# Host layouts, split input weights, idle matmuls and a new step order at the head of a hybrid decoder layer

## The chip, the cores and the metric

The kernel runs on one core of one Trainium2 chip. The metric is the time of one execution on the device in microseconds (us), smaller is better. Arrays that the host lays out before the launch are not in it.

The names of the engines in the profile: PE is TensorE (matmuls; PEld its weight loads), DVE VectorE, ACT ScalarE, POOL GpSimd, SP the engine that issues nearly all DMAs. SPq, ACTq and so on are the instruction queues of these engines. L127 is line 127 of the kernel.

## What is computed

One layer of a decoder trunk, for 2048 prompt rows and 64 sample rows (8 sequences of 8 positions), with shared weights, all in float32:

```
h = rmsnorm(x, g_pre_mix)
q, k, v, u = split(h @ w_in)              # 1024 -> 512 + 128 + 128 + 512 columns
attn   = window attention of rope(q), rope(k), v, window 128, one sink logit per head
pooled = (trailing mean of u over 2/4/8/16 positions - u) @ pool_w, times pool_scale
mix = concat(rmsnorm(attn, g_attn_out), rmsnorm(pooled, g_pool_out)) @ w_out
x += rmsnorm(mix, g_post_mix)
x += rmsnorm(relu(rmsnorm(x, g_pre_mlp) @ w_up)**2 @ w_down, g_post_mlp)
x += sigmoid(x @ w_ple_gate + b) * (p @ w_ple)
```

The sample rows attend to 128 past keys and values per sequence (state_k, state_v), and their pooling starts from the last 15 pooled inputs (state_pool). New keys, values and pooled inputs are outputs as well.

## The kernel before, in words

Every float32 product is made of three products of split operands (mm3, L132 to L136): an operand is rounded to a shorter format (its high part, a copy on ScalarE) and what is left is its low part (a subtraction on VectorE, lo_of, L129). high x high, high x low and low x high are added up in PSUM. So a weight matrix has to be loaded, scaled, copied and subtracted before it can be multiplied.

The first 440 us or so hold everything up to the input of w_out. The rows come in tiles of 128; the 64 sample rows are tile -1, the prompt rows tiles 0 to 15.

*Loading and splitting.* queue (L125) is a DMA that keeps its place in the order of SP's queue. load_gains (L286) loads norm weights as eight rows of 128, turns them with a TensorE transpose (gps, L296) and copies them into gains: the eight columns of g_pre_mix at the start, the eight of g_attn_out and g_pool_out in tile 2. load_w_in (L320) loads 128 rows of w_in with all 1280 columns (raw, six buffers), scales them by g_pre_mix and writes the high part (L324, ScalarE) and the low part (L325, VectorE). head (L347) loads the rows x of a tile, their transposed form xt, and the rotary table cs, and forms the norm factor; split_head (L370) splits xt into hT.

*front* (L380) is a tile's product with w_in, in eight steps of 128 rows (k): kvps (keys and values, 256 columns), qps (512), ups (512), then rotary work, transposes of keys and queries (trk, trq) and copies. For tile -1 the three products run together, step by step, as w_in arrives. Its past keys (sk) and pooled inputs (su) are turned on TensorE (trk L660 in sample_attention, trs L571 in pooling).

*attention* (L485) works in six steps (a): scores and softmax for each of two key groups, then for each group the transposes of the weights (trp, L541) with their split (pt), and the product with the values (po, L551 and L552). *pooling* (p) has three steps, *finish* (l) two. *split_w_out* (e, L751) loads w_out in pieces (wraw), scales them by g_attn_out or g_pool_out (L767, L768; wsp has one buffer) and stores the split form in device memory (wod); it belongs to tiles 3 to 10.

*The order of the work.* The main loop weaves, for each tile t, the attention and pooling of t with the front of t + 1 (f) and the finish of t - 1. A string of letters says in which order the next steps are taken: ORDER (L44) for tiles 0 to 2 and 11 to 13, called plain tiles here, ORDERW (L46) for tiles 3 to 10, ORDER1 and ORDER2 for 14 and 15. What this gives is the program's order; the framework then places instructions on each engine's queue by its own model of time, so that an instruction whose inputs it takes to be ready can be put ahead of one that stands earlier in the program. On the chip each queue is worked off in order.

After this part come the product with w_out, the two large products with w_up and w_down, and the gate; the change does not touch them.

Of the kernel before, what the change touches and what calls it, by code (L numbers as in the profile page):

```python
# [10 lines left out]
F32 = mybir.dt.float32  # L11
# [3 lines left out]
ALU = mybir.AluOpType  # L15
PSUM = bass.MemoryType.PSUM

P = 128
# [7 lines left out]
HD = 64  # L26
# [16 lines left out]

ORDER = "a f f f l f a f f p a f f f f f a f p f a f f l f p a"  # L44

# [43 lines left out]
def trunk(ctx: ExitStack, tc: tile.TileContext, i: dict, o: dict):  # L89
# [184 lines left out]
    with ExitStack() as sa:  # L274
# [10 lines left out]

        def load_gains(names, c0):  # L286
            graw = pa.tile([8, P], F32, tag="r", bufs=1, name="graw", padded_shape=[8, 512])
            r = 8 // len(names)
            for k, name in enumerate(names):
                rows = graw[k * r : (k + 1) * r]  # L290
                if name == "g_attn_out":
                    queue(rows.rearrange("k (g p) -> k g p", g=2), i[name][0].rearrange("(g k p) -> k g p", g=2, p=HD))
                else:
                    queue(rows, i[name][0].rearrange("(k p) -> k p", p=P))
            gps = tr.tile([P, 8], F32, tag="tr", name="gps", padded_shape=[P, 512])
            T.transpose(gps, graw, ident[:8, :8])  # L296
            V.tensor_copy(gains[:, c0 : c0 + 8], gps)

# [20 lines left out]

        def load_w_in(k):  # L320
            raw = over.pool.tile([P, INC], F32, tag="raw", bufs=6, name="raw")
            queue(raw, w_in[k * P : (k + 1) * P, :])
            g = gpre[:, k : k + 1]
            A.mul(out=wi[k][:, 0], in_=raw, mul=g)  # L324
            V.scalar_tensor_tensor(out=wi[k][:, 1], in0=raw, scalar=g, in1=wi[k][:, 0].bitcast(F32), op0=ALU.mult, op1=ALU.subtract)  # L325

        def load_pool_w():
            raw = over.pool.tile([P, INC], F32, tag="raw", bufs=6, name="raw")
            pr = raw[:, 0:512].rearrange("p (g d) -> p g d", g=4)
            SY.dma_start(pr, i["pool_w"][0].rearrange("g c d -> c g d"))  # L330
            SY.dma_start(raw[:, 512:1024], i["pool_scale"].to_broadcast([P, 512]))
            V.tensor_tensor(out=pr, in0=pr, in1=raw[:, 512:1024].rearrange("p (g d) -> p g d", g=4), op=ALU.mult)
            A.copy(out=pw[:, 0], in_=pr)
            lo_of(pw[:, 1], pr, pw[:, 0])
# [45 lines left out]
        def front(t, hT, cs, rs, res):  # L380
# [62 lines left out]
            yield  # L443
            if t >= 0:
                ups = mmp.tile([P, 512], F32, tag="mm", name="ups")
            for j, _ in enumerate(gemm(768, 512, ups) if t >= 0 else ()):
                yield
                if j == 0:
                    kp = over.pool.tile([P, 4, 256], F32R, tag="kp", bufs=2, name="kp")
# [110 lines left out]
        def pooling(t, u, mix, sq):  # L560
# [5 lines left out]
            if t < 0:  # L566
                sp = past[2]
                ns = NDEC * HALO
                ps = tr.tile([P, 4, P], F32, tag="tr", name="trs")
                for g in range(4):  # L570
                    T.transpose(ps[:, g, :ns], sp[:ns, g * P : (g + 1) * P], ident[:ns, :ns])  # L571
                V.tensor_copy(ux[:, :, :, :HALO], ps[:, :, :ns].rearrange("p g (b j) -> p g b j", b=nb))
            elif t == 0:
# [63 lines left out]

        def load_past():
            sp = over.pool
            sks = []  # L640
            for j in range(2):
                sk = sp.tile([P, 4, P], F32, tag="sk", bufs=2, name="sk")
                queue(sk, i["state_k"][0, 4 * j : 4 * j + 4].rearrange("b s g d -> s b (g d)"))
                sks.append(sk)
            su = sp.tile([P, 512], F32, name="su")
            queue(su[: NDEC * HALO], i["state_pool"][0].rearrange("b j c -> (b j) c"))
            sv = sp.tile([P, NDEC, P], F32, tag="raw", bufs=6, name="sv", padded_shape=[P, NDEC, 160])
            queue(sv, i["state_v"][0].rearrange("b s g d -> s b (g d)"))
            return sv, sks, su

        def sample_attention(kr, vr, qr, mix, sq):
            n = NS
            sp = over.pool
            sv, sks, _ = past
            kT = sp.tile([P, NDEC, P], F32, tag="raw", bufs=6, name="kT", padded_shape=[P, NDEC, 160])
            for j in range(2):
                sk = sks[j]
                ps = tr.tile([P, 4, P], F32, tag="tr", name="trk")
                for c in range(4):
                    T.transpose(ps[:, c, :], sk[:, c, :], ident)  # L660
# [129 lines left out]
        for t in range(-1, NT):  # L790
# [725 lines left out]
```

## Time and profile before

| | us |
|---|---|
| median of three runs | 2169.63 |
| lowest, highest | 2165.42, 2170.01 |
| the profiled execution, its own time | 2167.38 |
| span of its profile (first to last instruction) | 2165.6 |
| TensorE busy in it | 2127.1 |
| VectorE busy | 1581.1 |
| ScalarE busy | 958.5 |

The profile is of one execution. "Busy" of an engine is time in which an instruction of it runs; a matmul's end is modelled, and consecutive matmuls overlap, so that the distance from one start to the next tells their pace better than their durations. A wait is put down to the instruction whose signal came last. Rows in order of time give start, duration, engine, line, operation, out <- in, shapes and count, and in brackets the idle time of the engine before and what ended it.

### The profile page before, as it was taken

How to read it: one execution, taken by the hardware profiler on the slowest of the kernel's cores; microseconds unless marked ns; L12 is line 12 of the kernel's file. 1: busy time of each engine (PE TensorE's matmuls, PEld its weight loads, DVE VectorE, ACT ScalarE, POOL GpSimd, SP SyncE). 2: the span in 40 equal slices, each digit the busy share in tenths (PEclk: the TensorE clock that was granted, in tenths of full speed). 3: DMA queues.
4: the chain of work that ended last, by engine and by line, in shares of the span. 5: the costliest groups of instructions: out<-in, count | busy, mean ns of one | idle time of the engine just before them, and what ended most of it. 6: DMA issues, size and time to landing. Idle time of an engine off the chain costs nothing.

```text
span 2165.6 us, 31185 instructions
## 1 busy us (share of the span) xinstructions
PE 2127.1 (98%) x11435; PEld 1879.0 (87%) x11435; DVE 1581.1 (73%) x2716; ACT 958.5 (44%) x1856; POOL 566.7 (26%) x642
## 2 busy tenths in 40 slices
PE   8999999899999999999999999999999999999999
PEld 6888888777889999999999988788888888888887
DVE  6789999866688777555755566788888888876553
ACT  4667666635455445444544455233233233232221
POOL 2334443233341000000000035535535544300000
PEclk9999999999999999999999999999999999999999
DMA  6254312667879768766766632322231232342211
GB/s 209 75 178 164 96 62 89 238 209 219 258 247 309 239 211 272 206 192 187 228 199 191 180 111 78 111 84 65 90 100 49 90 100 62 117 138 83 88 54 40
DMA packets 309634, 320.43 MB, mean 148 GB/s; under 512 B 79526, under 2 KB 257906, under 8 KB 302281
## 3 DMA queue, kind: packets, MB, share of 16 engines
q1 hardware_dynamic: 309481, 318.44, 46.6%
q8 instruction: 90, 1.47, 0.3%
q14 instruction: 63, 0.52, 0.1%
HBM read 217.17 MB, written 102.51 MB: 148 GB/s over the span
## 4 chain that ended last, share of the span: by engine, by line
PE 81%; DVE 7%; DMA 4%; issue 3%; POOL 3%; ACT 2%; SPq 1%; POOLq 0%; ACTq 0%; DVEq 0%
PE up L1060 9%; PE up L1062 9%; PE up L1061 9%; PE dn L1276 9%; PE dn L1278 9%; PE dn L1277 9%; PE pg L136 3%; PE pg L135 3%; PE pg L134 3%; PE ups L134 1%; PE ups L136 1%; PE ups L135 1%; PE qps L135 1%; PE qps L134 1%; PE qps L136 1%
## 5 line engine op out<-in xcount | busy, mean ns | idle before, releaser
L1286 DVE TENSOR_TENSOR z<-dn,z 128x512 f32<-128x512 f32 x416 | 278.0, 684 | 77.7 <-PE dn L1278 69.8
L130 DVE TENSOR_TENSOR g<-raw,g 128x512 fp32r<-128x512 f32 x336 | 226.9, 694 | 89.6 <-ACT g L207 88.7
L1060 PE MATMUL up<-e,g 128*128 128x352 f32 x832 | 269.8, 325 | 5.1 <-ACT snap L1067 5.0
L1061 PE MATMUL up<-e,g 128*128 128x352 f32 x832 | 268.3, 322 | 0.0
L1062 PE MATMUL up<-e,g 128*128 128x352 f32 x832 | 264.5, 324 | 0.0
L207 ACT CAST g<-raw 128x512 fp32r<-128x512 f32 x336 | 203.9, 623 | 97.8 <-PE up L1062 78.0
L1225 POOL TENSOR_TENSOR raws<-raws 128x1024 f32<-128x1024 f32 x32 | 83.9, 2632 | 615.7 <-DVE wr L130 408.5
L1276 PE MATMUL dn<-wr,ms 128*128 128x512 f32 x512 | 199.3, 390 | 1.4 <-DVE z L1286 1.4
L1277 PE MATMUL dn<-wr,ms 128*128 128x512 f32 x512 | 199.2, 389 | 0.0
L1278 PE MATMUL dn<-wr,ms 128*128 128x512 f32 x512 | 198.2, 389 | 0.0
L1060 PEld LDWEIGHTS up<-e,g 128*128 128x128 f32 x832 | 157.0, 189 | 6.1 <-ACT snap L1067 5.6
L1061 PEld LDWEIGHTS up<-e,g 128*128 128x128 f32 x832 | 157.8, 190 | 0.1
L1062 PEld LDWEIGHTS up<-e,g 128*128 128x128 f32 x832 | 156.0, 189 | 0.0
L1074 DVE TENSOR_TENSOR t<-up,snap 128x352 f32<-128x352 f32 x144 | 71.3, 520 | 114.7 <-ACT snap L1067 101.0
L207 ACT CAST m<-fr 128x512 fp32r<-128x512 f32 (+1 forms) x128 | 65.4, 514 | 194.2 <-PE dn L1278 169.2
L1276 PE MATMUL dn<-wr,m 128*128 128x512 f32 x384 | 149.5, 389 | 1.7 <-DVE z L1286 1.7
L1277 PE MATMUL dn<-wr,m 128*128 128x512 f32 x384 | 149.4, 389 | 0.0
L1278 PE MATMUL dn<-wr,m 128*128 128x512 f32 x384 | 149.3, 389 | 0.0
L856 POOL TENSOR_TENSOR s<-fr 128x256 f32<-128x256 f32 x64 | 54.1, 845 | 309.6 <-DVE ms L130 238.7
L1067 ACT COPY snap<-up 128x352 f32<-128x352 f32 x144 | 61.0, 454 | 165.7 <-PE up L1062 165.6
L207 ACT CAST wr<-raws 128x1024 fp32r<-128x1024 f32 x66 | 69.2, 1052 | 114.7 <-PE dn L1278 57.8
L1276 PEld LDWEIGHTS dn<-wr,ms 128*128 128x128 f32 x512 | 96.1, 188 | 21.8 <-issue 1.8
(285 smaller groups left out, 5707.6 us busy)
## 6 DMA issues: line engine op xcount, KB each, us to landing
raw<-in_w_up_dram SPq DMA_DIRECT2D x160, 256.0 KB, 3.9
raw<-upt SPq DMA_DIRECT2D x32, 1024.0 KB, 7.9
fr<-ffd SPq DMA_DIRECT2D x64, 512.0 KB, 3.5
ffd<-r SPq DMA_DIRECT2D x96, 256.0 KB, 2.7
upt<-raw SPq DMA_DIRECT2D x16, 1024.0 KB, 5.2
raws<-in_w_down_dram SPq DMA_DIRECT2D x32, 512.0 KB, 5.4
sp<-hfd SPq DMA_DIRECT2D x21, 704.0 KB, 6.2
x<-in_x_prompt_dram SPq DMA_DIRECT2D x16, 512.0 KB, 4.5
```

The source lines that it names most:

```text
L130: eng.tensor_tensor(out=out, in0=full, in1=hi.bitcast(F32), op=ALU.subtract)
L134: T.matmul(ps, lhs[0], rhs[0], start=first, stop=False)
L135: T.matmul(ps, lhs[0], rhs[1], start=False, stop=False)
L136: T.matmul(ps, lhs[1], rhs[0], start=False, stop=last)
L207: copy(out=dst[:, 0], in_=src)
L1060: T.matmul(ps, l[0], r[0], start=st, stop=False, skip_group_check=not fresh)
L1061: T.matmul(ps, l[0], r[1], start=False, stop=False, skip_group_check=not fresh)
L1062: T.matmul(ps, l[1], r[0], start=False, stop=c == 3, skip_group_check=not fresh)
L1276: T.matmul(ps, l[0], r[0], start=fresh and j == 0, stop=False, skip_group_check=not fresh)
L1277: T.matmul(ps, l[0], r[1], start=False, stop=False, skip_group_check=not fresh)
L1278: T.matmul(ps, l[1], r[0], start=False, stop=j == 1, skip_group_check=not fresh)
L1286: V.tensor_tensor(out=z, in0=ps, in1=z, op=ALU.add)
```

## The change

- The host lays out three things: all sixteen columns of norm weights in one array (gains_t), the past keys transposed (state_kt), and the past pooled inputs transposed (state_pt). The kernel loads each with one DMA; load_gains and the transposes trk (L660) and trs (L571) with their copies are gone. The past pooled inputs are copied into place by GpSimd instead of VectorE.
- w_in is loaded in two column parts per 128 rows: columns 0 to 767 (q, k, v) of all eight row blocks first, then columns 768 to 1279 (u). raw has nine buffers of 768 columns instead of six of 1280.
- The transposed sample rows are loaded in two halves, between the first pieces of w_in.
- For tile -1 kvps and qps run together, ups afterwards.
- spin: before the first load is there, TensorE makes 18 transposes of the identity into a PSUM tile that nobody reads.
- The transposed rows of tile 0 are loaded ahead of its rows x, with the past keys, the constants and the sinks in between; past pooled inputs and values come after.
- ORDER is another string.

```diff
-ORDER = "a f f f l f a f f p a f f f f f a f p f a f f l f p a"
+ORDER = "f f f f l f a f f p a f f f f f a f p f a f f l a a p"
...
+        queue(gains, i["gains_t"])
+
+        def spin(k):
+
+            ps = tr.tile([P, 4, P], F32, tag="tr", name="spin")
+            for j in range(k):
+                T.transpose(ps[:, j % 4, :], ident, ident)
...
-        def load_w_in(k):
-            raw = over.pool.tile([P, INC], F32, tag="raw", bufs=6, name="raw")
-            queue(raw, w_in[k * P : (k + 1) * P, :])
+        def load_w_in(k, part):
+
+            c0, cw = (0, 768) if part == 0 else (768, 512)
+            raw = over.pool.tile([P, cw], F32, tag="raw", bufs=9, name="raw", padded_shape=[P, 768])
+            queue(raw, w_in[k * P : (k + 1) * P, c0 : c0 + cw])
             g = gpre[:, k : k + 1]
-            A.mul(out=wi[k][:, 0], in_=raw, mul=g)
-            V.scalar_tensor_tensor(out=wi[k][:, 1], in0=raw, scalar=g, in1=wi[k][:, 0].bitcast(F32), op0=ALU.mult, op1=ALU.subtract)
+            hi, lo = (wi[k][:, h, c0 : c0 + cw] for h in range(2))
+            A.mul(out=hi, in_=raw, mul=g)
+            V.scalar_tensor_tensor(out=lo, in0=raw, scalar=g, in1=hi.bitcast(F32), op0=ALU.mult, op1=ALU.subtract)
...
             if t < 0:
+                for j in range(2):
+                    js = slice(4 * j, 4 * j + 4)
+                    queue(xt[:, js, :n], x_t[:, js, c0 : c0 + n])
+                    load_w_in(j, 0)
+                for k in range(2, 5):
+                    load_w_in(k, 0)
+            if t == 0:
                 queue(xt[:, :, :n], x_t[:, :, c0 : c0 + n])
-                for k in range(2):
-                    load_w_in(k)
+                load_past(0)
+                queue(ct, i["consts"])
+                load_sinks()
             x = fp.tile([P, D], F32, tag="x", bufs=1, name="x")
             queue(x[:n], xrows(t))
-            if t >= 0:
+            if t > 0:
                 queue(xt[:, :, :n], x_t[:, :, c0 : c0 + n])
...
-                ups = op.tile([P, 512], F32, tag="o", name="ups")
-                for _ in zip_longest(gemm(512, 256, kvps, 1), gemm(0, 512, qps, 1), gemm(768, 512, ups, 1)):
+                for _ in zip_longest(gemm(512, 256, kvps, 1), gemm(0, 512, qps, 1)):
                     pass
...
-                for g in range(4):
-                    T.transpose(ps[:, g, :ns], sp[:ns, g * P : (g + 1) * P], ident[:ns, :ns])
-                V.tensor_copy(ux[:, :, :, :HALO], ps[:, :, :ns].rearrange("p g (b j) -> p g b j", b=nb))
+                G.tensor_copy(ux[:, :, :, :HALO], past["u"].rearrange("p g (b j) -> p g b j", b=nb))
...
-            for j in range(2):
-                sk = sks[j]
-                ps = tr.tile([P, 4, P], F32, tag="tr", name="trk")
-                for c in range(4):
-                    T.transpose(ps[:, c, :], sk[:, c, :], ident)
-                V.tensor_copy(kT[:, 4 * j : 4 * j + 4, :], ps)
-                yield
+            kT, sv = past["k"], past["v"]
...
-        load_gains(["g_pre_mix"], 0)
+        spin(18)
         heads[-1] = head(-1)
         split_head(-1)
-        for k in range(2, 8):
-            load_w_in(k)
+        for k in range(5, 8):
+            load_w_in(k, 0)
+        for k in range(8):
+            load_w_in(k, 1)
         heads[0] = head(0)
-        past = load_past()
-        queue(ct, i["consts"])
-        load_sinks()
+        load_past(1)
...
-            if t == 2:
-                load_gains(["g_attn_out", "g_pool_out"], 8)
```

More of the change, by code (lines that the diff above doesn't have):

```diff
@@ L284, in trunk @@
         mmp = sw.enter_context(tc.tile_pool(name="mmp", bufs=2, space=PSUM))
[L286 to L297, printed above, removed]
+        queue(gains, i["gains_t"])
[3 more added lines that the diff above has]
+                T.transpose(ps[:, j % 4, :], ident, ident)
         ct = ca.tile([P, C_COLS], F32, name="ct")
@@ L443, in front @@
             yield
-            if t >= 0:
-                ups = mmp.tile([P, 512], F32, tag="mm", name="ups")
-            for j, _ in enumerate(gemm(768, 512, ups) if t >= 0 else ()):
+            ups = mmp.tile([P, 512], F32, tag="mm", name="ups") if t >= 0 else op.tile([P, 512], F32, tag="o", name="ups")
+            for j, _ in enumerate(gemm(768, 512, ups)):
                 yield
+                if t < 0:
+                    continue
                 if j == 0:
@@ L636, in finish, with load_past @@
             SY.dma_start(mixd[t], mix[:, :, :n])
-        def load_past():
+        past = {}
+        def load_past(part):
             sp = over.pool
-            sks = []
-            for j in range(2):
[L642 to L649, printed above, removed]
+            if part == 0:
+                past["k"] = sp.tile([P, NDEC, P], F32, name="kT")
+                queue(past["k"], i["state_kt"])
+                return
+            past["u"] = sp.tile([P, 4, NDEC * HALO], F32, name="su")
+            queue(past["u"], i["state_pt"])
+            past["v"] = sp.tile([P, NDEC, P], F32, name="sv")
+            queue(past["v"], i["state_v"][0].rearrange("b s g d -> s b (g d)"))
         def sample_attention(kr, vr, qr, mix, sq):
@@ L1504 @@
     given["p_t"] = np.ascontiguousarray(p_all.T)
+    g_pre, g_attn, g_pool = (given.pop(n)[0] for n in ("g_pre_mix", "g_attn_out", "g_pool_out"))
+    g_attn = g_attn.reshape(2, 4, HD).transpose(0, 2, 1).reshape(P, 4)
+    given["gains_t"] = np.ascontiguousarray(np.concatenate([g_pre.reshape(8, P).T, g_attn, g_pool.reshape(4, P).T], axis=1))
+    given["state_kt"] = np.ascontiguousarray(given["state_k"][0].reshape(NDEC, WIN, P).transpose(2, 0, 1))
+    given["state_pt"] = np.ascontiguousarray(given["state_pool"][0].reshape(NDEC * HALO, 4, P).transpose(2, 1, 0))
     del given["p_prompt"], given["p_sample"]
```

14 lines of the change are left out of this document (4 added, 10 removed).

## The prediction

> **What bounds the kernel now.** I read the page first, then the waits of TensorE, then the busy time by stretches of the first 404 us, and then the first 27 us in order of time. The page shows one engine near its limit:
>
> ```profile
> span 2165.6 us, 31185 instructions
> PE 2127.1 (98%) x11435; PEld 1879.0 (87%) x11435; DVE 1581.1 (73%) x2716; ACT 958.5 (44%) x1856; POOL 566.7 (26%) x642
> L1225 POOL TENSOR_TENSOR raws<-raws 128x1024 f32<-128x1024 f32 x32 | 83.9, 2632 | 615.7 <-DVE wr L130 408.5
> ```
>
> TensorE (PE) is busy for 2127.1 of 2165.6 us, so no edit outside its idle 38.5 us gains unless it shortens TensorE's own work. The waits say where the idle time is (columns: who waited for whom, us in all, times, longest):
>
> ```profile
> PE kvps L134 <- ACT wi L324: 5.2, 1, 5.2
> ...
> PE trp L541 <- DVE pr L531: 3.9, 1, 3.9
> ...
> PE trk L453 <- DVE pt L130: 2.2, 1, 2.2
> PE trp L541 <- ACT vp L426: 1.7, 1, 1.7
> ...
> PE ups L134 <- DVE es L525: 1.2, 1, 1.2
> ...
> PE po L552 <- DVE pt L130: 0.6, 2, 0.3
> ```
>
> The stretches place them (columns: stretch, PE, PEld, DVE, ACT, POOL busy, granted clock, DMA share, GB/s):
>
> ```profile
> 52.00:100.00 48.00, 48.00 (x295) 41.92 (x293) 34.86 (x122) 29.03 (x82) 19.02 (x27) 1.00 0.31 87
> 100.00:140.00 40.00, 40.00 (x257) 35.54 (x256) 36.36 (x92) 26.91 (x68) 13.98 (x16) 1.00 0.41 138
> 140.00:148.00 8.00, 5.08 (x26) 3.67 (x25) 7.94 (x27) 6.78 (x19) 4.71 (x7) 1.00 0.90 287
> 148.00:317.00 169.00, 168.19 (x1064) 148.33 (x1063) 156.28 (x424) 118.16 (x300) 66.83 (x85) 1.00 0.35 114
> 317.00:388.00 71.00, 70.93 (x453) 62.78 (x452) 64.05 (x181) 46.57 (x126) 27.29 (x36) 1.00 0.31 103
> 388.00:404.00 16.00, 9.82 (x49) 8.46 (x48) 14.81 (x36) 10.44 (x27) 6.31 (x8) 0.68 1.02 411
> ```
>
> So the change can touch three places: the start; a stall of 8 - 5.08 = 2.9 us at 140 to 148 (the 1.7 and 1.2 us waits), where VectorE (DVE) is full, in the tiles whose order is rewritten; and the TensorE transposes that it removes. Between 148 and 388 TensorE loses 0.9 us in 240. The 6.2 us lost at 388 to 404 belong to the last two tiles, whose orders stay.
>
> **The start.** In order of time (columns: start, duration, engine, line, what, idle time before it):
>
> ```profile
> 1.12 0.29 POOL L110 TENSOR_SCALAR_AFFINE_SELECT ident<-ident 128x128 f32<-128x128 f32 x1
> 4.14 0.71 ACT L376 CAST hT<-xt 128x256 fp32r<-128x256 f32 x2 [2.13 <-DMA xt<-in_x_t_dram]
> 6.39 1.36 ACT L324 ACTIVATE wi<-raw,gains 128x1280 fp32r<-128x1280 f32 x1 [1.55 <-DMA raw<-in_w_in_dram]
> 7.81 0.47 PE L134 MATMUL kvps<-wi,hT 128*64 128x256 f32 x1 [5.23 <-ACT wi L324]
> 10.73 0.63 PE L135 MATMUL ups<-wi,hT 128*64 128x512 f32 x1
> 11.16 0.63 PE L136 MATMUL ups<-wi,hT 128*64 128x512 f32 x1
> 13.90 9.48 DVE L325 SCALAR_TENSOR_TENSOR wi<-raw,gains,wi 128x1280 fp32r<-128x1280 f32 x6 [0.38 <-ACT wi L324]
> 14.35 0.40 PE L136 MATMUL ups<-wi,hT 128*64 128x512 f32 x1
> 20.17 0.28 PE L134 MATMUL kvps<-wi,hT 128*64 128x256 f32 x1
> 20.42 1.37 ACT L324 ACTIVATE wi<-raw,gains 128x1280 fp32r<-128x1280 f32 x1 [0.23 <-DMA raw<-in_w_in_dram]
> 21.90 0.28 PE L134 MATMUL kvps<-wi,hT 128*64 128x256 f32 x1
> 23.54 1.15 ACT L376 CAST hT<-xt 128x512 fp32r<-128x512 f32 x2 [0.59 <-DMA xt<-in_x_t_dram]
> 25.13 0.40 PE L136 MATMUL ups<-wi,hT 128*64 128x512 f32 x1
> 25.36 1.31 PE L660 MATMUL trk<-ident,sk 128*128 128x128 f32 x8
> 26.42 0.36 PE L134 MATMUL kvps<-wi,hT 128*128 128x256 f32 x1
> 33.59 0.63 PE L571 MATMUL trs<-ident,su 120*128 120x120 f32 x4
> ```
>
> *First product.* Today x^T lands at 4.14 and the first 655 KB of w_in 2.25 us later. The change asks for half of x^T and 768 of the 1280 columns. The piece then takes 0.6 of 2.25 us, 1.35; half of x^T less in front brings it forward by about 0.6. That is 4.14 - 0.6 + 1.35 = 4.9 us; ScalarE's (ACT) split takes 0.6 x 1.36 = 0.8, so TensorE starts near 5.8 instead of 7.81.
>
> *How soon the input product of the sample rows can end* (today 25.36). Three bounds:
> - TensorE: one row block of w_in costs 21.90 - 20.17 = 1.73 us at full speed, eight cost 13.8: 5.8 + 13.8 = 19.6, plus what is lost at half speed.
> - VectorE: six low parts take 9.48, 1.58 each, and eight 12.6: 5.8 + 12.6 = 18.4; rotary work on these rows comes between, and 3 us of it would still fit under the next bound.
> - The load: the last piece is waited for until 20.42 today, and the same bytes stand ahead of it. The last piece is then 512 columns: 0.4 x 1.37 + 0.4 x 1.58 + 0.4 for the last products gives 22.0.
>
> I take the highest, 22.0. The load feeds ScalarE and VectorE piece by piece, and both stay faster than it. Sixteen pieces instead of eight cost SP more issues, but SP is ahead of the data; nine smaller slots hold 3.5 MB where six held 3.9, and the tenth piece waits for a low part that is done near 7. Bounds: 20.7, TensorE's own with the loss below, and 24, if narrow pieces stream a tenth slower.
>
> *The idle matmuls.* The clock shows in the pitch: 0.43 us from 10.73 to 11.16 for 512 columns, about 0.23 from 25.13 to 25.36; the first short matmul is that at 14.35, 6.5 us after the first product. Later the clock falls once more:
>
> ```profile
> 392.83 1.60 PE L541 MATMUL trp<-ident,pr 128*128 128x128 f32 x8 [3.94 <-DVE pr L531]
> ...
> 398.66 0.77 PE L551 MATMUL po<-pt,vp 128*128 128x512 f32 x1
> ...
> 403.74 0.39 PE L135 MATMUL pab<-wo,ms 128*128 128x512 f32 x1
> ```
>
> There, work is back at full pace by 403.74, at most 5.1 us after the first real matmul at 398.66. Eight transposes took 1.60 us, so 18 take 3.6: from 1.45, when the identity is ready, to 5.1, and the products follow at 5.8. If they open the clock, it opens 5.1 to 6.5 us after 1.45, at 6.6 to 8.0; the products lose at most (8.0 - 5.8) / 2 = 1.1 us, TensorE's bound is 20.7 and stays under 22.0. If only real matmuls open it, that is at 10.9 to 12.3: a loss of 2.6 to 3.3 and a bound of 22.2 to 22.9. The price of the difference is up to 0.9 us, since the load covers the rest.
>
> The Trainium skill, "TensorE: Matmul & The Clock Gate", section "Part 4: PE-mode transpose", says that transposes do not count as activity for the clock; the spin consists of transposes, so by that rule it does nothing and the second case holds. The trace does not decide: counted from the transposes at 392.83 the return takes 10.9 us, but there was an idle stretch of 2.2 us among them.
>
> *What follows at once.* The product of tile 0 needs hT of tile 0, which waited for x^T until 23.54; the 512 KB of x ahead of it now come after it. At 655 KB in 1.58 us that is 1.25 us: 22.3, plus half of 1.15 for the first cast, 22.9. Tile 0's first product moves from 26.42 to 22.9, a gain of **3.5 us**; the eight transposes of past keys (25.36 to 26.42) are within it. Bounds: 21.9 (4.5) and 24.5 (1.9).
>
> *Other removals.* Four transposes of pooled features: 0.45 of their 0.63 us, the rest overlaps what follows. The transpose of the second gains, below: 0.2. Together **0.6**. The halo copy that goes to GpSimd (POOL) is 480 columns, by the 2632 ns for 1024 about 1.2 us; tile 0's products cover it, uncovered it would cost 1.2. The copies that VectorE loses (keys, features, gains) are priced at nothing, the queue being covered.
>
> **The steps of plain tiles and the stall at 140.** Here the least visible part of the change acts:
>
> ```profile
> L762 SPq DMA_DIRECT2D wraw<-in_w_out_dram x16: 465/546/1843, 54.4 to 172.2; - x16
> L767 ACT ACTIVATE wsp<-wraw,gains x16: 706/722/729, 110.1 to 211.5; 128x512 fp32r<-128x512 f32 x16
> ...
> L296 PE MATMUL gps<-ident,graw x2: 223/232/240, 2.3 to 109.0; 8*128 8x8 f32 x2
> ...
> 118.94 4.55 DMA wod<-wsp
> ```
>
> w_out is loaded from 54.4, yet its first scaling (L767) is at 110.1, right after the gains are turned at 109.0 in tile 2. From there its pieces, one buffer each waiting for a store (4.55 us in the chain), sit in the in-order queues of ScalarE and VectorE, and the stall at 142 is in that stretch. With all gains there from the start the pieces can begin about 55 us earlier, in 52 to 100, where VectorE is free for 48 - 34.86 = 13.1 us; six low parts of 512 columns, at 0.4 x 1.58, need 3.8. I take the stall as gone: **2.9 us**. Bounds: it is only moved (0), or a like one is added (-2.9).
>
> The order itself moves attention one step later and lets its last two steps follow each other (a a p). I price it at nothing: tiles 3 to 10 already end in a a l, and in 148 to 317 TensorE loses 0.8 us of 169; the waits row for po holds 0.6.
>
> **Sum.** 3.5 + 0.6 + 2.9 = 7.0 us, 0.32%. The profiled execution took 2167.38 us (span 2165.6 and 1.8 around it): 2160.4. The median of the three runs, 2169.63, lies 2.25 above it: 2162.6.
>
> **Rivals**, on the median's base:
> - *The stall stays or moves* (VectorE as full as at 140): 4.1 us, 2165.5. For it: VectorE is busy 36.36 of 40 at 100 to 140, and the in-order queues stay. Against: 13.1 free us before. Chance 0.25.
> - *Transposes do not open the clock*: 0.9 less, 2163.5. For it: the 10.9 us above. Against: the idle stretch among them. Chance 0.13.
> - *Narrow pieces arrive slower*: tile 0 begins at 24.5: 1.9 + 0.6 + 2.9 = 5.4, 2164.2. For it: one row of a piece has 3 or 2 KB where it had 5. Against: today's x^T, in rows of 256 bytes, is there by 4.14. Chance 0.08.
> - *Slower: the uncovered a a.* After the last transposes ScalarE casts and VectorE subtracts before po can run:
>
> ```profile
> L130 DVE TENSOR_TENSOR pt<-trp,pt x32: 661/680/693, 150.5 to 318.4; 128x512 fp32r<-128x512 f32 x32
> ...
> L543 ACT CAST pt<-trp x30: 564/587/632, 157.9 to 316.8; 128x512 fp32r<-128x512 f32 x30
> ```
>
> 0.59 + 0.59 + 0.68 = 1.9 us per tile with nothing between; six plain tiles: 11.2, less 4.1: 2176.7. It decides from 0.7 us per tile, and gives over 0.2% from 1.4. Against it stands the same ending in tiles 3 to 10. Chance 0.08.
> - The forecast keeps 0.46.
>
> **Numbers.** 0.2% is 4.3 us, about what a measurement of this kernel can tell from no change; the bound is 2165.3. The forecast lies within reach of it only at its upper bounds (0.9 of 0.46 faster), the first rival sits on it (0.4 of 0.25), the second is mostly faster (0.8 of 0.13), the third too (0.6 of 0.08): 0.66 faster. Slower takes 0.08 and 0.02 for an added stall; 0.24 is left. The range: down to 2156.5, where the start reaches its better bound (1.0 more) and the 6.2 us at 388 to 404 happen to shrink by most; up to 2169.5, where start and stall both take their worse values and the run lies 2 us high.
>
> **What would show it.** First real product near 5.8 and pitch of 0.23 for 512 columns by 8; tile 0's kvps near 22.9; no trk and trs groups before it; first L767-type scaling near 55 to 60; TensorE above 39.8 of 40 in the stretches up to 150. The forecast is wrong if the pitch changes after 10.5, if scaling begins early and a wait for pr, es or vp over 1 us remains in tiles 0 to 3, or if po waits add up to more than 2 us.

## The result, and the profile after

The changed kernel takes 2155.97 us (median of 6 runs, 2151.88 to 2158.03), the kernel before 2168.9 us in runs taken beside it (6 runs, 2165.42 to 2172.86): a ratio of 0.994 with a 95% interval of 0.9929 to 0.9951. It is faster, as forecast, but by 12.9 us where 7.0 was forecast, and it lies 0.5 us under the range. The profiled execution took 2156.64 us, its span is 2154.9: 10.7 less than the span before. The accounts by stage below are of single executions, and about 2 of the 12.9 us are not in them.

The head of the page after:

```profile
span 2154.9 us, 31214 instructions
PE 2129.8 (99%) x11439; PEld 1882.8 (87%) x11439; DVE 1573.8 (73%) x2719; ACT 956.8 (44%) x1864; POOL 576.3 (27%) x643
```

TensorE's busy time has not shrunk; its idle time has, from 38.5 to 25.1 us. The stretches after (columns as in the prediction: stretch, PE, PEld, DVE, ACT, POOL busy, granted clock, DMA share, GB/s):

```profile
0.00:30.00 30.00, 24.16 (x112) 15.62 (x113) 18.89 (x39) 18.44 (x26) 7.14 (x16) 1.00 0.93 286
30.00:60.00 30.00, 29.34 (x196) 24.36 (x195) 15.62 (x50) 11.86 (x34) 9.69 (x16) 0.89 0.54 160
...
100.00:140.00 40.00, 40.00 (x254) 35.56 (x254) 33.80 (x91) 25.24 (x66) 12.19 (x16) 1.00 0.56 184
140.00:148.00 8.00, 8.00 (x48) 6.88 (x46) 7.91 (x26) 7.36 (x21) 5.48 (x6) 1.00 0.95 313
...
388.00:404.00 16.00, 12.62 (x78) 11.16 (x76) 14.73 (x49) 12.94 (x37) 6.69 (x9) 0.79 0.99 395
...
440.00:540.00 100.00, 100.00 (x478) 82.03 (x477) 69.00 (x64) 52.55 (x85) 43.66 (x55) 1.00 0.75 229
```

The stretches of before that the prediction did not show:

```profile
0.00:30.00 30.00, 21.94 (x103) 14.70 (x104) 18.96 (x27) 17.31 (x19) 5.55 (x18) 1.00 0.99 305
30.00:60.00 30.00, 30.00 (x224) 24.65 (x223) 17.95 (x64) 11.72 (x31) 9.68 (x15) 1.00 0.42 126
...
440.00:540.00 100.00, 95.06 (x447) 76.63 (x447) 62.42 (x60) 45.29 (x76) 35.01 (x50) 1.00 0.73 216
```

Three things are to be seen. The stall at 140 to 148 is gone (8.00 of 8.00, where it was 5.08). The start is *slower*: in the first 60 us TensorE runs 308 matmuls, 18 of them the idle transposes, where before ran 327, and the granted clock is 0.89 in the second half. (The record of the clock begins with its first opening, at 10.07 us in after and at 14.33 in before. For what lies ahead of that the column shows 1.00, though the pitch of 0.43 us in the prediction's rows is that of half speed.) And 440 to 540 is now full: 478 matmuls where before had 447, in a stretch of code that the change does not touch.

Busy time hides a slow clock, so the rest is counted otherwise. "Lost by T" is T less the useful work that TensorE has begun by then: every matmul is counted at the pitch that its shape has at full clock, back to back (0.227 us for 512 columns, 0.120 for 256, and so on, medians of the trace); the idle transposes and the transposes that the change removes count as no work. The pitches are medians, so a figure can come out a little below zero; what counts is the difference between rows. What each stage loses, in us, for both kernels and those of the experiments:

```
kernel                  0-60  60-380  380-440  440-540  540-640  rest   time
before                  15.4    4.4    11.9      6.6      8.1     8.1   2168.9
after                   20.5   -0.3     7.6      0.7      7.8     7.3   2155.97
e1 after, old order     22.6    4.8     8.5      1.9      7.6     8.7   2165.05
e4 after, no spin       21.2   -0.1     7.6      0.7      9.2     8.6   2157.53
e5 after, 60 spins      18.6    8.0     9.2      8.2      6.9     7.8   2167.83
e8 after, x late        18.9    3.4     8.0      0.7      8.1    10.7   2157.15
e9 after, whole rows    16.1   13.3     8.4      0.5      5.7    10.1   2171.5
e2 before, new order    15.8    2.4     9.2      8.2      7.5     8.3   2164.59
e3 before, gains        14.7   13.2     9.2      0.9      8.5     6.6   2166.26
e7 before, both         14.7    8.9     9.4      7.5      8.4     6.7   2169.2
```

Between after and before: the start gives up 5.1 us, the plain tiles (60 to 380) win 4.7, and at 380 the two are level (20.2 and 19.8 lost). The whole net gain comes behind that, at 380 to 540: 4.3 and 5.9 us. So the question became: what decides the stretch 380 to 540, which the change leaves alone?

### The profile page after: what moved, and what is told of

Same layout as the page of the kernel before. It is cut to its first block, busy times and chain, and to the rows that moved or that the text cites. A ratio compares the mean times of both kernels' runs of the same rounds, so it can differ in the third digit from the quotient of the medians.

```text
span 2154.9 us, 31214 instructions
## 1 busy us (share of the span) xinstructions
PE 2129.8 (99%) x11439; PEld 1882.8 (87%) x11439; DVE 1573.8 (73%) x2719; ACT 956.8 (44%) x1864; POOL 576.3 (27%) x643
```

## The experiments

**Parts of the change, one by one.** The kernel's program gives an order of steps, but the framework that builds it places each instruction on its engine by its own model of time. An edit at the start can therefore move instructions anywhere behind it.

*e1_old_order* is the changed kernel with the old step order of plain tiles:

```diff
-ORDER = "f f f f l f a f f p a f f f f f a f p f a f f l a a p"
+ORDER = "a f f f l f a f f p a f f f f f a f p f a f f l f p a"
```

> The changed kernel with the old order string; everything else stays. If the new order carries the gain of 13 us (theory 1: it removes the stall near 140 and lets attention run ahead of the front), this takes 2163 to 2169 us, TensorE stalls again by 2 us or more between 100 and 260, and po of tile 14 ends after 410 us. If the gains that are there from the start carry it (theory 2: w_out is scaled from tile 0 on), it stays at 2154 to 2158 and no such stall comes back.

Measured: 2165.05 us, ratio to before 0.9982 (0.9972 to 0.9992). Losses of 5 us are back between 100 and 200.

*e2_new_order* is the reverse: the kernel before, with the new order alone.

> The kernel before with the new order string alone. Theory 1: 2155 to 2161, the stall at 140 to 148 gone, and since the start stays that of before (5 us better than the changed one's up to 60 us), possibly below the changed kernel. Theory 2: 2166 to 2170, the stall at 140 stays.

Measured: 2164.59 us, 0.9976 (0.9966 to 0.9986). Neither theory's range holds it. The order, priced at nothing in the prediction, is worth 4.4 us alone, and 9.1 on top of the other parts (2165.05 less 2155.97), with the new placement that comes with it.

*e3_gains* is the kernel before with all gains laid out by the host and loaded at the start, which lets the scaling of w_out begin early:

```diff
-        load_gains(["g_pre_mix"], 0)
+        queue(gains, i["gains_t"])
...
-            if t == 2:
-                load_gains(["g_attn_out", "g_pool_out"], 8)
```

> The kernel before with all norm weights loaded from the host's array at the start, nothing else: w_out can be scaled from tile 0 on. Theory 2: first scaling at 55 to 65 us, the stall at 140 gone, 2158 to 2164. Theory 1: within 2 us of the kernel before, a stall of 2 us or more somewhere between 60 and 260.

Measured: 2166.26 us, 0.9986 (0.9977 to 0.9995). The scaling does begin at 59.0 us, as in the changed kernel (60.0; it was 110.1):

```profile
L767 ACT ACTIVATE wsp<-wraw,gains x16: 707/723/738, 59.0 to 163.3; 128x512 fp32r<-128x512 f32 x16
```

and yet TensorE loses 13.1 us between 100 and 200, more than the 3.7 of before. So the early scaling does not remove the stall by itself.

*e7_order_gains* has both edits, e2's and e3's.

> The kernel before with the new order and all norm weights from the host's array; its start (w_in in whole rows, transposes of past keys on TensorE, no idle matmuls) stays. If order and early gains together are the gain and the new start is a loss, this is faster than the changed kernel: at 60 us it has lost 5 us less of TensorE's time, no stall over 1 us lies between 60 and 380, and the time is 2149 to 2155. If the new start is needed for the gain further on, it stays at 2158 to 2165.

Measured: 2169.2 us, 0.9999 (0.999 to 1.0007): the two gains of 4.4 and 2.7 us do not add up but vanish, 9.1 us being lost between 100 and 200 and 7.5 at 440 to 540.

Not all of these losses are waiting. In most of the traces with a stall at 100 to 200 the granted clock is halved behind it: for 3.41 us in e2 and e7, and in e5 and e8 below, for 10.24 in e9, and for 13.65 in e3. Half of that is lost while TensorE works, so up to 6.8 of e3's 13.1 us are slow clock. The profile of before shows no such halving behind its stall at 140, but those of e10, e11 and e14 do, 3.41 us from 145.59, 147.77 and 145.82, though their engines work in the same order as before's until 417 us. The three lose 1.8 to 4.0 us more than before at 60 to 380. So single profiles of one order differ by that much, before's is the best of its four, and what the plain tiles win is rather more than 4.7.

*e4_no_spin* is the changed kernel without the idle transposes (the line `spin(18)` is taken out). Apart from them the order of instructions on TensorE, ScalarE and VectorE is that of the changed kernel.

> The changed kernel without the 18 idle transposes. If transposes count as work for the clock, the first short matmuls come 3 us or more later after the first product than in the changed kernel (there at 10.1, 3.4 after the first product), and the time rises by 0 to 2 us. If they do not count, the pace changes 3.4 to 6.8 us after the first product, as a matter of where the product falls, and the time is the same within 1 us.

Measured: 2157.53 us, 0.9949 (0.9937 to 0.9961), 1.6 us over the changed kernel with overlapping intervals. The clock opens at 14.1 instead of 10.1 us, and 0.7 us more are lost by 60.

*e5_spin60* has 60 idle transposes instead of 18.

> The changed kernel with 60 idle transposes instead of 18, so that they outlast two of the stretches in which the clock could open. If transposes count for the clock, their pitch falls from 0.213 to 0.109 us within the row of 60, 3.4 to 6.8 us after its start at 1.5, and it is over by 10 us. If they do not count, all 60 keep 0.213, the row lasts 12.8 us to 14.3, and the pace changes only after real matmuls.

Measured: 2167.83 us, 0.9991 (0.9981 to 1.0002). The row of transposes in after, and in e5 with what follows it:

```profile
1.47 4.10 PE L292 MATMUL spin<-ident 128*128 128x128 f32 x18 [1.47 <-POOL ident L110]
```

```profile
1.46 8.83 PE L292 MATMUL spin<-ident 128*128 128x128 f32 x60 [1.46 <-POOL ident L110]
...
10.48 0.40 PE L134 MATMUL qps<-wi,hT 128*64 128x512 f32 x1
10.72 0.39 PE L135 MATMUL qps<-wi,hT 128*64 128x512 f32 x1
```

Eighteen take 4.10 us, 0.228 each; sixty take 8.83, 0.147 each: the pitch falls from 0.213 to 0.109 us within the row, and the products behind it run at 0.23 us from the first on. The clock opened at 5.73 us, with nothing run but transposes. Eighteen can be enough: with the same row of 18 the clock opened at 5.39, 5.33 and 4.39 us in e1, e16 and e17, ahead of the first product, and in e17 the row itself became shorter:

```profile
1.47 3.59 PE L292 MATMUL spin<-ident 128*128 128x128 f32 x18 [1.47 <-POOL ident L110]
```

The rule that the prediction weighed (the Trainium skill, "TensorE: Matmul & The Clock Gate", "Part 4: PE-mode transpose": transposes do not count as activity for the clock) does not hold for these transposes. But 42 more instructions at the start also gave another placement, with 7.4 us lost at 100 to 200 and 8.2 at 440 to 540. This edit costs nothing where it is made (18.6 us lost by 60, against 20.5), and the time moved by 12 us.

**The start.** *e8_x_late* is the changed kernel with the loads of x and of the rotary table for the sample rows behind all of w_in.

> The changed kernel with the rows x and the rotary rows of the sample tile loaded after all of w_in. In the kernels before and after, the packets of w_in take twice as long or more just in the 3 us in which the packets of x and of the rotary rows run (7 to 10 and 10 to 13 us). If these packets slow the rest, the slow stretch moves behind w_in, the last piece of w_in is split 1.5 to 3 us earlier and the product u of the sample rows ends at 25 to 26 instead of 27.6; time 2153 to 2156. If the slow stretch comes from elsewhere, w_in is slowed near 10 to 13 us all the same and the time stays within 1 us of the changed kernel.

Measured: 2157.15 us, 0.9943 (0.9929 to 0.9957). The load at 10 to 15 us, first of after, then of e8 (last column GB/s):

```profile
10.00:15.00 5.00, 4.16 (x21) 2.18 (x20) 3.06 (x3) 3.00 (x6) 0.00 (x0) 1.00 1.02 237
```

```profile
10.00:15.00 5.00, 5.00 (x28) 3.52 (x27) 4.87 (x5) 4.78 (x7) 0.00 (x0) 1.00 1.04 401
```

The queues are busy in both (1.02, 1.04), but while x is among the loads they move 237 instead of 401 GB/s. By 20 us e8 has lost 8.6, after 11.6, and the input product of the sample rows ends at 23.2 instead of 27.6; the last matmul of it, first in after, then in e8:

```profile
27.25 0.39 PE L136 MATMUL ups<-wi,hT 128*64 128x512 f32 x1
```

```profile
22.82 0.40 PE L136 MATMUL ups<-wi,hT 128*64 128x512 f32 x1
```

The 3 us do not reach the end: what now comes late keeps TensorE waiting at 20 to 30 us, the clock halves at 27.50 for 3.41 us, so that 1.6 are left by 60 us, and 3.5 are lost between 100 and 200.

*e9_whole_rows* is the changed kernel with w_in loaded in whole rows again and the three products of the sample rows in one pass, as before.

> The changed kernel with w_in in whole rows and the three products of the sample rows run together, as before; idle matmuls, host layouts and order of the changed kernel stay. If the column parts make the new start slow, u of the sample rows ends at 24 to 25.5 us, TensorE has lost 2 to 4 us less at 60 us, and the time is 2151 to 2154. If they do not, it is 2156 to 2160, with the first product later by 1 us.

Measured: 2171.5 us, 1.0009 (0.9998 to 1.0021). By 60 us it has lost 16.1, against 20.5 in after and 15.4 in before. By 45 us 1.5 of the 4.4 us are there: that is what the cut into two column parts with its separate products costs. The rest is the clock at 51 us (below), which in e9 stays up. The cut alone does not slow the load: over the first 15 us the queues move 227 GB/s in after (212 to 265 in six more kernels whose loads come in the same order), 273 in before, 275 in e9 and 289 in e8. Only narrow pieces with x among them come slower; why is open. e9's placement then loses 12.6 us at 100 to 200, up to 5.1 of them slow clock.

**The stretch 440 to 540.** What the kernels that lose little there have in common shows in SP's queue (start, duration, queue, line). Before, around the first residuals:

```profile
432.10 0.58 SPq L230 DMA_DIRECT2D mr<-mixd  x1
432.82 0.56 SPq L636 DMA_DIRECT2D mixd<-mix  x1
437.47 0.32 SPq L230 DMA_DIRECT2D mr<-mixd  x1
437.84 0.42 SPq L178 DMA_DIRECT2D g_post_mix<-in_g_post_mix_dram  x1
...
448.92 0.33 SPq L884 DMA_DIRECT2D x1d<-xt  x1
```

After:

```profile
425.69 0.32 SPq L637 DMA_DIRECT2D mixd<-mix  x1
429.60 0.60 SPq L230 DMA_DIRECT2D mr<-mixd  x1
430.28 0.61 SPq L178 DMA_DIRECT2D g_post_mix<-in_g_post_mix_dram  x1
...
434.76 0.33 SPq L230 DMA_DIRECT2D mr<-mixd  x1
440.30 0.33 SPq L876 DMA_DIRECT2D x1d<-xt  x1
```

In before the load of tile 4's mr stands ahead of g_post_mix. It has to wait for its buffer, from 433.4 to 437.47, and SP with it; so g_post_mix is issued at 437.84, and the first residual, which needs it, is late. In before VectorE waits 6.1 us for g_post_mix, and TensorE waits as follows between 425 and 540 us (in after it has no such wait there):

```profile
PE pab L134 <- ACT z L252: 3.0, 3, 1.8
PE trx L896 <- DVE ez L886: 1.5, 1, 1.5
```

Counted by useful work done when g_post_mix is issued, the kernels above fall into two groups: in after, e1, e3, e4, e8 and e9 TensorE has done 401.1 to 402.4 us of work by then, and they lose 0.5 to 1.9 us at 440 to 540; in before, e2, e5 and e7 it has done 406.3, and they lose 6.6 to 8.2. The theory (P in the records): this late load is the cause. The rival (Q): it only stands beside it, and the order on ScalarE and VectorE, which goes with it, makes the loss.

*e10_gpost_first* and *e12_order_gpost* fix the order of these loads in the kernel before, alone and with the new step order:

```diff
-        r = into.tile([P, D], F32, name=name)
-        SY.dma_start(r, i[name].to_broadcast([P, D]))
+        r = into.tile([P, D], F32, name=name); d = SY.dma_start(r, i[name].to_broadcast([P, D]))
+        tc.keep_in_program_order(d) if name in ("g_post_mix", "g_pre_mlp") else None
...
-            raw = self.mrp.tile([P, 8, P], F32, tag="mr", bufs=2, name="mr")
-            SY.dma_start(raw[:, :, :n], mixd[t])
+            raw = self.mrp.tile([P, 8, P], F32, tag="mr", bufs=2, name="mr"); d = SY.dma_start(raw[:, :, :n], mixd[t])
+            tc.keep_in_program_order(d) if t == 4 else None
```

> The kernel before, with one load moved: SP issues the loads of g_post_mix and g_pre_mlp ahead of the load of mr of tile 4 (in the kernel before SP waits for that load's buffer until 437.47 and issues g_post_mix at 437.84; the changed kernel issues it at 430.3). Instruction orders up to 430 us are those of before. Theory P (the place of this load decides the stretch 440 to 540, where before loses 7.8 us and the changed kernel 0.8): the wait of DVE ez for g_post_mix, 6.1 us, goes, TensorE loses 5 to 7 us less at 440 to 540, and the kernel takes 2162 to 2164 us against 2169. Theory Q (the load only stands beside it; ScalarE's and VectorE's order, which stays nearly the same here, makes the loss): 2167 to 2170.

> The kernel before with the new step order of plain tiles (2164.59 us alone) and with g_post_mix loaded ahead of tile 4's mr. Theory P: it loses up to 8 us less at 440 to 540, 2157 to 2160 us; with the start of before, 5 us better than that of the changed kernel, it comes near the changed kernel, 2156, or beats it. Theory Q: 2163 to 2166.

Measured: 2187.88 us, 1.0083 (1.0068 to 1.0098), and 2180.43 us, 1.0055 (1.0041 to 1.0068): much slower. The waits of e10 between 425 and 540 say why:

```profile
PEld pab L134 <- ACT ms L207: 20.4, 1, 20.4
PE pab L134 <- ACT ms L207: 20.2, 1, 20.2
```

The edit moved the load of tile 4's mr far back, behind the residual chain (to 485 us in e10), and TensorE waited 20 us for that tile. The two runs changed two things and do not tell the theories apart.

*e11_three_mr* gives mr three buffers instead of two (`bufs=3`) in the kernel before.

> The kernel before with three buffers for mr instead of two: the load of tile 4's mr no longer waits for its buffer, so that g_post_mix, still behind it on SP, is issued by about 434 instead of 437.84. Theory P: 4 to 7 us faster than before, 2162 to 2165. Theory Q: 2167 to 2170.

Measured: 2177.12 us, 1.004 (1.0027 to 1.0054). With the third buffer the load of tile 5's mr moved ahead of g_post_mix too and waited in the place of tile 4's: g_post_mix at 442.54, again after 406.3 us of work, and 11.4 us lost at 440 to 540. The wait had not been taken away, so this says nothing against P; it agrees with it.

*e13_gpost_twice* goes the other way: the changed kernel with g_post_mix loaded twice into its tile, so that the reader waits for the second landing.

> The changed kernel with g_post_mix loaded twice into the same tile, so that its reader waits for the second landing, near 440 instead of 435. Theory P: the changed kernel then loses 3 to 7 us more at 440 to 540: 2159 to 2163 us against 2156. Theory Q: within 1.5 us of 2156.

Measured: 2166.3 us, 0.9986 (0.9978 to 0.9995), 10.3 us over the changed kernel. 440 to 540 now loses 8.7 us instead of 0.7, with up to 440 nothing changed but 0.9 us. The only long wait of TensorE there, behind which the clock is halved for 6.83 us:

```profile
PE pab L134 <- ACT z L252: 5.4, 1, 5.4
```

That agrees with P, but it does not rule out Q: from 436 us on the edit also changed the order of instructions on all four engines.

*e14_mr_by_act* is the clean test. In the kernel before, the load that makes SP wait is issued by ScalarE; TensorE keeps its order but for one matmul, VectorE and GpSimd wholly:

```diff
-            SY.dma_start(raw[:, :, :n], mixd[t])
+            (A if t == 4 else SY).dma_start(raw[:, :, :n], mixd[t])
```

> The kernel before; the load of mr of tile 4, for whose buffer SP waits until 437.47, is issued by ScalarE instead. Every engine keeps its order of instructions, but for one matmul on TensorE. g_post_mix is issued near 433.5 instead of 437.84. Theory P (the late load starts the chain of residuals late and TensorE pays for it): VectorE's first scaling by g_post_mix starts at 439.6, when its rsq is ready, instead of 443.58; TensorE loses 3 to 5 us less than 7.8 at 440 to 540; 2164 to 2166 us against 2169. Theory Q (the instruction orders alone make the loss): within 1 us of 2169.

Measured: 2166.2 us, 0.9985 (0.9976 to 0.9994). SP's queue in e14, and VectorE's first use, in before and then in e14:

```profile
434.18 0.57 SPq L636 DMA_DIRECT2D mixd<-mix  x1
434.80 0.42 SPq L178 DMA_DIRECT2D g_post_mix<-in_g_post_mix_dram  x1
...
446.08 0.33 SPq L884 DMA_DIRECT2D x1d<-xt  x1
```

```profile
443.58 1.28 DVE L882 SCALAR_TENSOR_TENSOR ez<-ez,rsq,g_post_mix 128x1024 f32<-128x1024 f32 x1 [6.06 <-DMA g_post_mix<-in_g_post_mix_dram]
```

```profile
441.41 1.28 DVE L882 SCALAR_TENSOR_TENSOR ez<-ez,rsq,g_post_mix 128x1024 f32<-128x1024 f32 x1 [2.54 <-ACT z L252]
```

e14 runs 1.4 us behind before at this point, and still its first x1d is stored 2.8 us earlier. It loses 2.3 us at 440 to 540 where before loses 6.6: 4.3 less, as theory P had it (3 to 5), with the orders that Q holds responsible left as they were. The time shows 2.4 of it: in e14's profile 1.4 were lost earlier and 0.5 later, the 1.4 where both have the same order.

*e15_order_mr_act* is the same edit on e2 (new step order alone).

> The kernel before with the new step order (2164.59 alone, 8.2 us lost at 440 to 540) and tile 4's mr issued by ScalarE. All orders on TensorE, VectorE and GpSimd are those of the new step order alone. Theory P: 3 to 5 us less lost there, 2159.5 to 2161.5. Theory Q: within 1 us of 2164.6.

Measured: 2160.19 us, 0.9965 (0.9953 to 0.9978), 4.4 us under e2's 2164.59; 440 to 540 loses 5.1 where e2 lost 8.2. All four engines keep e2's order throughout. P holds a second time, though the stretch is not as full as in after: the clock is halved for 3.41 us from 520.84, as it is in e2 from 522.74.

**The clock at 51 us.** In after the clock halves at 51.03 for 6.83 us while TensorE is busy without a gap:

```profile
47.18 0.64 PE L725 MATMUL pos<-ptn,vr 64*64 64x256 f32 x2
47.75 1.12 PE L728 MATMUL pos<-pts,sv 128*64 128x32 f32 x16
48.80 0.64 PE L725 MATMUL pos<-ptn,vr 64*64 64x256 f32 x2
49.37 1.12 PE L728 MATMUL pos<-pts,sv 128*64 128x32 f32 x16
50.42 0.30 PE L134 MATMUL pq<-rr,pw 128*128 128x64 f32 x1
...
52.83 0.41 PE L136 MATMUL kvps<-wi,hT 128*128 128x256 f32 x1
53.05 0.41 PE L134 MATMUL kvps<-wi,hT 128*128 128x256 f32 x1
...
58.03 0.28 PE L134 MATMUL kvps<-wi,hT 128*128 128x256 f32 x1
58.15 0.28 PE L135 MATMUL kvps<-wi,hT 128*128 128x256 f32 x1
```

The same matmul has a pitch of 0.22 us at 52.83 and of 0.12 at 58.03. The halving falls into an unbroken block of 48 narrow matmuls, from 47.18 to 52.47; narrow means here 32 or 64 columns, or operands of 64 rows. In every trace the changes of the clock lie whole multiples of 3.41 us apart (here 51.03 - 10.07 = 12 x 3.41), as if time were cut into intervals of that length, and one of them, 47.62 to 51.03, lies wholly within the block. The same holds in all six kernels whose clock halves there (after, e1, e4, e5, e8, e13). In e9 the same 48 matmuls run at full clock, take 4.6 us, and cover at most 2.6 us of one interval. In before and the kernels made from it the block has 36 matmuls and 3.2 us, too short for a whole interval, and the clock stays.

The theory (N): such a block halves the clock. The rival (T): something else at that time does.

*e16_pq_early* and *e17_pos_split* break the block by another step order of the sample rows, e16 first:

```diff
-ORDER0 = "f a f a a p a a p a a f f f a f p f"
+ORDER0 = "f a f p a a p a a p a a f f f a f f"
```

```diff
-ORDER0 = "f a f a a p a a p a a f f f a f p f"
+ORDER0 = "f a f a a a a p a a f f f a f p f p"
```

> The changed kernel with the pooling step of the sample rows ahead in the step order, so that the narrow pq matmuls no longer follow pos: no narrow block longer than 3.3 us. Theory N (an unbroken block of narrow matmuls halves the clock): the clock stays at 1.00 between 40 and 70 us, and TensorE has lost 17 to 18 us by 60 us instead of 20.5. Rival T (something else at that time, a transfer or a wide window of low load, halves it): 0.50 within 48 to 62 again. The total is open, since later orders change: 2150 to 2166.

> The changed kernel with the attention steps of the sample rows ahead, so that the pos matmuls fall into two groups with wide matmuls between them, and pq follows the second group after one wide matmul: no unbroken narrow block over 3.5 us. Theory N: clock 1.00 between 40 and 70, 17 to 18 us lost by 60 us. Rival T: 0.50 again. Total open: 2150 to 2166.

Measured: e16 2170.34 us, 1.0004 (0.9995 to 1.0013); e17 2157.08 us, 0.9954 (0.9939 to 0.9969). The clock in the stretch 44 to 62, in after, e16 and e17 (column before the last two):

```profile
44.00:62.00 18.00, 18.00 (x112) 15.57 (x111) 7.45 (x22) 6.48 (x14) 3.31 (x6) 0.81 0.38 103
```

```profile
44.00:62.00 18.00, 18.00 (x120) 14.55 (x119) 6.53 (x19) 5.84 (x12) 4.50 (x7) 1.00 0.41 113
```

```profile
44.00:62.00 18.00, 18.00 (x133) 15.13 (x132) 10.65 (x31) 7.50 (x16) 6.30 (x11) 1.00 0.40 108
```

Both keep the full clock there, and by 60 us they have lost 16.3 and 18.3 instead of 20.5. Theory N holds: two different ways of breaking the block both keep the clock. How full an interval has to be is not settled. In e17 the clock halves at 35.11 for 3.41 us, without a gap in TensorE's work, behind 2.9 us of other narrow matmuls (the scores of the sample rows, scs, from 31.57 on), which fill only 2.7 us of the interval, whereas in before 3.2 us of the block above did not halve it. Neither total is better: e16's placement loses 8.2 us at 60 to 380 and belongs to the late group at 440 to 540 (406.3 us of work at the load, 5.7 lost); e17's loses 4.0 at 60 to 380 and belongs to the early group. No kernel tried beats the changed one beyond the intervals.

## Why the prediction was wrong

*First product at 5.8.* It came at 6.71. x^T's half landed at 4.6, not 3.5, and the first part of w_in at 5.72, not 4.9; the split took 0.93, about as reckoned (0.8).

```profile
4.64 0.41 ACT L382 CAST hT<-xt 128x256 fp32r<-128x256 f32 x1 [2.64 <-DMA xt<-in_x_t_dram]
5.72 0.93 ACT L322 ACTIVATE wi<-raw,gains 128x768 fp32r<-128x768 f32 x1 [0.67 <-DMA raw<-in_w_in_dram]
```

*The input product of the sample rows ends at 22.0.* This is the step that failed most: it ended at 27.6, 2.1 later than before (25.5) instead of 3.5 earlier. ScalarE's last casts of w_in, and VectorE's queue behind them:

```profile
21.24 1.93 ACT L322 ACTIVATE wi<-raw,gains 128x512 fp32r<-128x512 f32 x3
```

```profile
21.44 0.68 DVE L406 TENSOR_TENSOR qr<-qps,cs 64x512 f32<-64x512 f32 x1
22.04 0.74 DVE L409 TENSOR_TENSOR rb<-qps,cs 64x256 f32<-64x256 f32 x2
22.70 3.39 DVE L323 SCALAR_TENSOR_TENSOR wi<-raw,gains,wi 128x512 fp32r<-128x512 f32 x5
```

The casts of w_in end at 23.2, 1.4 us after the 21.8 at which those of before ended (20.42 + 1.37): the prediction had taken the same bytes to need the same time in any order, and with x among the narrow pieces they did not. What ended last was VectorE. The price of its parts was right: back to back, the low parts of 768 and 512 columns start 0.93 and 0.66 us apart, 1.59 for a row as against 1.58 whole. Wrong was that VectorE would start at 5.8 and work on without a wait, to end at 18.4 with room for 3 us of rotary work. Between 8 and 16 us it stood idle for 3.9 us, because pieces of w_in or x itself had not come, and from 16.20 on it never stood idle: eleven low parts take 8.1 us, and 1.7 us of rotary work comes in among them, now that the products for q, k and v end before that for u. Its last low part ends at 26.1. e8, where x and the rotary rows are loaded behind w_in, ends the product at 23.2, 1.2 over the forecast.

*Tile 0's product 3.5 us earlier.* Its first matmul runs at 25.61 instead of 26.42, but the next ones wait for the low parts, and by 60 us the kernel is 5.1 us behind: 2.0 by 45 us, and some 3 from the clock at 51 (half of 6.83), as e16 shows; the prediction had no such halving. The term was +3.5, with 0.45 more for the transposes of pooled inputs, and together they measured -5.1. That narrow pieces arrive slower was among the rivals. It came true in part: they do with x among them, and not in e8.

*The idle matmuls.* Right in the small: transposes open the clock (e5), and it is worth 0 to 1.6 us (e4). The time was not: 6.6 to 8.0 was forecast, and in after the clock opened at 10.07, 3.4 us after the first product. Whether 18 transposes open it ahead of the product differs between runs (they did in e1, e16 and e17). The rival that transposes do not count is refuted.

*Other removals, 0.6.* No run took them alone; beside the rest they are too small to be seen.

*The stall at 140 is gone, 2.9 us.* Right in size (5.08 of 8 became 8.00; 4.7 us at 60 to 380 with the smaller stalls at 220 to 250), and the scaling began at 60.0 as predicted. The reason given, that the scaling comes early, is not enough: e3 and e7 have it and lose 13 and 9 us at 100 to 200. What the runs show is that the stalls come and go with the placement as a whole, and that a halved clock behind them adds 1.7 to 6.8 us; what in the placement makes them stays open. So this term was right in size by luck.

*The order at nothing.* Wrong: alone 4.4 us (e2). The rival that feared uncovered attention steps is refuted too; waits of po are 0.7 us in all.

*Nothing behind 388.* This step put the time out of the range. The prediction left the 6.2 us at 388 to 404 where they were and looked no further, since the orders of those tiles stay; 380 to 540 gave 10.2 us. They do not stay as placed: TensorE idles 3.4 us there now, its wait of 3.9 us for pr is down to 0.7, and 440 to 540, where before idled 4.9 us, is full. The second is explained in its larger part by one load that no longer stands behind a waiting one (e13, e14, e15): 3 to 4 of the 5.9 us when only the queue is freed. The rest, and the first, are not settled.

So the direction was right by luck: the sum's two largest errors are opposite, -9.0 us at the start (5.1 lost where 3.9 were to be won), and +10.2 at 380 to 540, a place that the prediction put at nothing. Without the second the change would have been worth next to nothing.

## What to carry to other kernels

Where a framework places instructions by its own model of time, an edit anywhere can move the time by 10 us: give such an edit a range as wide as the stalls that the old placement shows, over the whole program. And read a difference of a few us between two single profiles only when more profiles of the same order bear it out. An in-order queue is read by what stands *behind* a wait: a load that waits for its buffer delays every load after it, and the one that a chain of work starts with should be ahead of it, or on another queue. Cutting a load into column parts is costed on the engine that works on the parts, with its waits for late pieces and with the work that can now come in between, and not on the load alone.

## What the runs showed of the hardware

- TensorE's clock halves though TensorE is busy without a gap, when an unbroken block of narrow matmuls fills a whole interval of 3.41 us (after: block from 47.18 to 52.47, clock 0.50 from 51.03 to 57.86, and so in five more kernels; block broken in e16 and e17: clock 1.00). One shorter block, 2.7 us of an interval, did it too (e17, at 35.11).
- A short wait can cost the clock behind it as well: in e14 it is halved for 3.41 us from 145.82 behind the stall at 140, in before it is not behind the same stall.
- Transposes alone open the clock: 60 of them ran at 0.147 us each on average where 18 took 0.228, with the clock open at 5.73 us, 4.3 us after the first.
- A full DMA share says little of the speed: 237 GB/s at a share of 1.02 while x of the sample rows is loaded among narrow pieces of w_in, 401 GB/s at 1.04 without it.
